# Two-layer hybrid decoder trunk on one core: a small tanh ahead of the gates, a swapped last step of the input projection, rotary key steps pinned, exponentials reordered

## The chip, the cores and the metric

The kernel runs on one core of one Trainium2 chip. The metric is the device time of one execution in microseconds (us), lower is better. The engines are named as in the profile: PE is TensorE (matmuls), DVE is VectorE, ACT is ScalarE, POOL is GpSimd, and SP issues the transfers.

## The reference

Two layers run over 256 tokens of width 1024. Each has a mixer sub-layer and a channel sub-layer; the change touches the mixer alone. Cut to what matters:

```
z = h @ w_in                        # one combined input projection of the normed x
q_lat, kv_lat, k_rope, qkv_b, conv_in, gate_logits = split(z)

q_a    = rms_norm(q_lat)  @ w_uq    # branch 1, MLA: 8 heads of 64 + 32 rotary
kv     = rms_norm(kv_lat) @ w_ukv
k_pe   = apply_rope(rms_norm(k_rope))                 # one rotary key, shared by the heads
o_a    = causal_attention(q_full, k_full, v_a) @ w_mla_o

o_b    = moba_attention(q_b, k_b, v_b) @ w_moba_o     # branch 2, here one block of 256 keys

glu_a, glu_g = split(conv_in)                         # branch 3, Conformer
u      = glu_a * sigmoid(glu_g)
u      = silu(layer_norm(causal_depthwise_conv(u, width 31)))
o_c    = u @ w_conv_pw2 + b

y      = (sigmoid(g0)*o_a + sigmoid(g1)*o_b + sigmoid(g2)*o_c) @ w_out
x      = x + g1 * y
```

`conv_in` is two times 512 channels wide. The latents (q_lat, kv_lat and k_rope) are together 672 wide. Sigmoid and silu are computed through tanh.

## The kernel before, in words

Every weight is float32 and is split by `split` into a rounded part (`whi`, made by ACT, L234) and a remainder (`wlo`, made by DVE, L235). A product then takes three matmuls (L324, L325, L327): `flush` issues the first two of every pair, and then the third of each. The weights come in units of up to 128x1024. `all_units` lists them in the order in which they are used, and `take` fetches and splits them a few units ahead of use (2 units in the input projection of layer 0, then 3). The four buffers `raw`, four `whi` and four `wlo` are taken in turn.

The code is written as one long sequence, but the order on each engine is drawn up when the kernel is built. A planner keeps one queue for each engine, follows the written order as a priority, and lets a later instruction go ahead where by its own estimate the earlier one's operands aren't there yet. What it drew up is fixed: on the chip each engine runs its list in order and waits where an operand is late. `tc.issue_after(i)` tells the planner to put an instruction behind `i` on the same engine.

The input projection of layer 0 is a loop over eight slices k of the model width. For each k, ACT and DVE make the normed and modulated slice: ACT `e` (L920) and its rounded copy `hh` (L921), DVE its remainder `hl` (L922). `latents(k)` multiplies it with the first 672 columns of the weights into three PSUM banks of the pool `psb` (`plat`, all three banks of the pool), and `conv_in(k)` with the 1024 columns of `conv_in` into four banks of the pool `psa` (`pci`, of five). `prepare_tile(k+1)` makes the next slice's gain and shift from 1024x1024 weights on DVE (L834) and is called between the two. At k = 2 the sine and cosine of the rotary angles are taken (L512), the only use of Sin. The other functions that ACT uses from there on are Tanh, Exp, Square, Copy and Identity.

After the loop, a written list of steps per layer, `STEPS`, sets the order. Layer 0 begins with `GLU0 GLU1 GLU2 GLU3 LE0 LE1 LR0 QKV00 LR1 LT QKV01 ...`:

- GLU: a tanh of one `pci` bank (L987, ACT) and its product with the other half (L988, DVE), into `upad`, the input of the width-31 convolution. It frees the bank.
- LE, LR, LT: the latents leave PSUM (L955 to L958, ACT), their squares are summed (L967, ACT) and raised to -1/2 (L545, POOL), and the latents are transposed (L975, PE) and split into the operands `qlh/qll` and `klh/kll` (L977 ACT, L978 DVE).
- QKV: the projection of the MoBA branch. Its first call takes two `psa` banks.
- UQ, UK, MS, MP: the up-projections of MLA, their norms, and the rotary steps. In `mla_prep` the shared rotary key `kr` is scaled (L1136) and turned (L1137, L1138, L678, L679).
- MA, BA: attention of four heads at a time through `attn4`. BA calls it with `apart=True`: the scores of the first 128 queries of heads 0 and 2 lie in a `psa` bank and those of heads 1 and 3 in a `psb` bank. Eight exponentials follow (L731, ACT), then two reciprocals (L736) and eight scalings (L743). The `p` buffers and the `smx` sums have four buffers each.
- V: the taps of the convolution (L1167, L1170, DVE), spread over most of the list; LN, LS, LB: the layer norm after it (L1180 to L1183 form its mean).
- C, G, O, OC, PR: gates and output projections; M and R: rows and columns of later modulations, from further weights (L432 on PE, L415 on DVE).

Layer 1 differs in that `conv_in` has the loop to itself and the latents follow as steps KL0 to KL7, behind the GLU steps.

Of the kernel before, what the change touches and what calls it, by code (L numbers as in the profile page):

```python
# [17 lines left out]
P = 128  # L18
# [142 lines left out]
def trunk_kernel(ctx, tc, xT, crow, ccol, pos, invf, modb_d, cols_d, grow_d, wmh, wmr, wm, win1, wqkv,  # L161
# [37 lines left out]
    def small(n, tag="sm", bufs=12):  # L199
        return wk.tile([P, n], F32, tag=tag, name=nm(tag), bufs=bufs)  # L200
# [60 lines left out]
    def all_units():  # L261
        for l in range(L):
            for k in range(KD):
                if l == 0:
                    yield win1[l, k, :, 0:672], [0], LEAD
                yield win1[l, k, :, 672:1696], [0], LEADS.get((l, "in", k), LEAD)
            for t in CFG["order"][l]:
                yield from ((*u, LEADS.get((l, *t), LEAD)) for u in token_units(l, t))
            if l == 1:
                for first in (0, NRAW):  # L270
                    for i in range(2):
                        for j in range(first, first + NRAW):
                            yield *chop(wup[l, j], KD, S)[i], LEADS.get((l, "up", j, i), LEAD)
            for up, j in FFN[l]:
                if up and l == 1 and j < 2 * NRAW:
                    continue
                for i, u in enumerate(chop(wup[l, j], KD, S) if up else chop(wdn[l, j], 1, 1024)):
                    yield *u, LEADS.get((l, "up", j, i), LEAD) if up else LEAD
# [403 lines left out]
    def attn4(qT, kT, v, scale, scq, oth, otl, oslot, apart=False):  # L682

        if apart:

            s0 = [psa(), psb()]
            at0 = [s0[h % 2][:, (h // 2) * P:(h // 2 + 1) * P] for h in range(4)]
        else:
            s0 = [psa()]
            at0 = [s0[0][:, (h % 2 * 2 + h // 2) * P:(h % 2 * 2 + h // 2 + 1) * P] for h in range(4)]  # L690
        s1 = [psa(), psa()]
        at1 = [s1[h % 2][:, (h // 2) * S:(h // 2 + 1) * S] for h in range(4)]
        for b, h in ((0, 0), (1, 1), (0, 2), (1, 3), (1, 0), (0, 1), (1, 2), (0, 3)):
            if b == 0:
                te.matmul(at0[h], qT(h)[:, 0:P], kT(h)[:, 0:P], start=(h == 0 or apart and h == 1), stop=False)
            else:
                te.matmul(at1[h], qT(h)[:, P:S], kT(h)[:, 0:S], start=(h < 2), stop=False)
        for t in s0:
            n = 2 if apart else 4
            te.matmul(t[:, 0:n * P].rearrange("p (h k) -> p h k", h=n), identb,  # L700
                      maskb.unsqueeze(1).to_broadcast([P, n, P]), start=False, stop=True)
        for t in s1:
            te.matmul(t.rearrange("p (h k) -> p h k", h=2)[:, :, P:S], identb,
                      maskb.unsqueeze(1).to_broadcast([P, 2, P]), start=False, stop=True)
        mx = small(8, "mx", 4).rearrange("p (b h) -> p b h", b=2)

        for i, t in enumerate(s0):
            n = 2 if apart else 4
            ve.tensor_reduce(mx[:, 0, n * i:n * i + n], t[:, 0:n * P].rearrange("p (h k) -> p h k", h=n), axis=AX.X,
                             op=ALU.max)  # L710
        for i, t in enumerate(s1):
            ve.tensor_reduce(mx[:, 1, 2 * i:2 * i + 2], t.rearrange("p (h k) -> p h k", h=2), axis=AX.X, op=ALU.max)
        nb = small(8, "nb", 4).rearrange("p (b h) -> p b h", b=2)
        if scq is None:
            ve.tensor_scalar(nb, mx, -scale, None, op0=ALU.mult)
        else:
            for b in range(NB):
                ve.scalar_tensor_tensor(nb[:, b, :], mx[:, b, :], -1.0, scq[b].rearrange("p (i j) -> p j i", i=2),
                                        op0=ALU.mult, op1=ALU.mult)
        yield  # L720
        prs = []
        for i in range(2):
            sm = small(4, "smx", 4)
            ps = []
            for h in (2 * i, 2 * i + 1):
                pr = wk.tile([P, 384], F32, tag="p", name=nm("p"), bufs=PB)
                for b in range(NB):
                    src = (at0 if b == 0 else at1)[h]
                    at = h % 2 * 2 + i
                    dst = pr[:, 0:P] if b == 0 else pr[:, P:384]  # L730
                    ac.activation(dst, src, AF.Exp, bias=nb[:, b, at:at + 1],  # L731
                                  scale=scale if scq is None else scq[b][:, h:h + 1],
                                  accum_out=sm[:, len(ps):len(ps) + 1])
                    ps.append(dst)
            ri = small(4, "ri", 4)
            ve.reciprocal(ri, sm)  # L736
            prs.append((ps, ri))
        for ps, ri in prs:
            for n, pr in enumerate(ps):
                if n in DVN:  # L740
                    ve.tensor_scalar(pr, pr, ri[:, n:n + 1], None, op0=ALU.mult)
                else:
                    ac.activation(pr, pr, AF.Copy, scale=ri[:, n:n + 1])  # L743
        yield
        pts = []
        slots = []
        for ps, _ in prs:
            slots += [ps[0], ps[1][:, 0:P], ps[1][:, P:S], ps[2], ps[3][:, 0:P], ps[3][:, P:S]]
            while len(slots) >= 4:
                pp = psa()  # L750
                for n in range(4):
                    te.transpose(pp[:, n * P:(n + 1) * P], slots[n], ident)  # L752
                slots = slots[4:]
                pt = operand([P, 512], "pT", "pT", 3, F32)
                ac.activation(pt, pp, AF.Copy)
                pts += [pt[:, n * P:(n + 1) * P] for n in range(4)]
        yield

        o = psa()
        for i in range(2):  # L760
            q0, q1 = slice(i * S, i * S + P), slice(i * S + P, i * S + S)
            for q, n, kb, start, stop in ((q0, 0, 0, True, True), (q1, 1, 0, True, False), (q1, 2, 1, False, True)):
                for j in range(2):
                    te.matmul(o[64 * j:64 * j + 64, q], v(2 * i + j, kb), pts[3 * (2 * i + j) + n], start=start,
                              stop=stop, tile_position=(0, 64 * j))
        oh = oth[:, oslot:oslot + 2, :].rearrange("p c t -> p (c t)")
        ac.activation(oh, o, AF.Copy)
        ve.tensor_tensor(otl[:, oslot:oslot + 2, :].rearrange("p c t -> p (c t)"), o, oh.bitcast(F32),
                         op=ALU.subtract)
# [27 lines left out]
    def layer(l):  # L797
# [112 lines left out]
        for k in range(KD):  # L910
            if l > 0:
                if k + 3 < KD:
                    tile(k + 3)
                hold[0] = [i.ins for i in tiles[-1]]
                conv_in(k)
                hold[0] = None
                mod_row(crow1[0], l, 2, k, scale=0.5 if CDMA else 1.0)
                continue
            t = e1()
            ac.activation(t, xn[k // 4][:, k % 4, :], AF.Identity, scale=gains[k], bias=sh1[:, k:k + 1])  # L920
            at = ac.activation(hh[:, k, :], t, AF.Copy)  # L921
            last = ve.tensor_tensor(hl[:, k, :], t, hh[:, k, :].bitcast(F32), op=ALU.subtract)  # L922
            if HOLD > 1:
                hold[0] = [last.ins]
            with tc.issue_after(wlast[0].ins) if k == 0 else ExitStack():
                latents(k)
            if k == 2:
                with tc.issue_after(at.ins):
                    step(trigs)
            if k + 1 < KD:  # L930
                prepare_tile(k + 1)
            conv_in(k)
            if k in C0K:
                gate_c(0, C0K[k], 3, psa)
            hold[0] = None
# [12 lines left out]
        qll = operand([P, 4, S], "lh1", "qll")  # L948
        klt = operand([P, 4, S], "obl", "klt")
        klh, kll = klt[:, 0:2, :], klt[:, 2:4, :]  # L950
        lats, lrs, krs = [], [], []

        def lat_evac(b):
            lat = ma(640)
# [15 lines left out]
        def lat_T():  # L970
            for n, gname, dh, dl, off in ((3, "q_g", qlh, qll, 0), (2, "kv_g", klh, kll, 384)):
                for c in range(n):
                    pt = psb()
                    for b in range(NB):
                        te.transpose(pt[:, b * P:(b + 1) * P], lats[b][:, off + c * P:off + (c + 1) * P], ident)  # L975
                    gcol = cv(l, gname)[:, c:c + 1]
                    ac.activation(dh[:, c, :], pt[:, 0:S], AF.Identity, scale=gcol)  # L977
                    ve.scalar_tensor_tensor(dl[:, c, :], pt[:, 0:S], gcol, dh[:, c, :].bitcast(F32),  # L978
                                            op0=ALU.mult, op1=ALU.subtract)


        upad = wk.tile([P, 4, S + 30], F32, tag="upad", name=nm("upad"), bufs=1)
# [136 lines left out]
        def mla_prep(b):  # L1119
# [13 lines left out]
            kf = ma().rearrange("p (h c) -> p h c", h=H)  # L1133
            ve.tensor_tensor(kf[:, :, 0:64], kn, krr.unsqueeze(2).to_broadcast([P, H, 64]), op=ALU.mult)
            kr = krs[b]
            ve.tensor_scalar(kr[:, 0:32], kr[:, 96:128], lrs[b][:, 2:3], None, op0=ALU.mult)  # L1136
            ve.tensor_tensor(kr[:, 32:64], kr[:, 0:32], ta[:, 0, b, 1, :], op=ALU.mult)  # L1137
            ve.tensor_tensor(kr[:, 64:96], kr[:, 0:32], ta[:, 1, b, 1, :], op=ALU.mult)  # L1138
            rope(kr[:, 0:16], kr[:, 16:32], kr[:, 32:64], kr[:, 64:96], 16)
# [454 lines left out]
```

## Time and profile before

| what | value |
|---|---|
| median of 3 runs | 900.23 us (899.14 to 901.38) |
| the profiled execution | 901.1 us, of which its span is 899.0 us |
| busy: PE, DVE, ACT, POOL | 877.8, 810.1, 557.8, 47.1 us |
| transfers | 201.59 MB, mean 224 GB/s |
| granted TensorE clock, mean | 0.996 |

The span is what the profiler recorded, from the first instruction of the program to its last. Busy time counts the stretches in which an engine has an instruction under way. An idle stretch is put down to what ended it. In the answers by time, each row is a start, a length, an engine, a line of the kernel, an operation and what it writes and reads; a bracket at the end gives the idle time ahead of it and who ended it.

### The profile page before, as it was taken

The page shows a single profiled execution, that of the slowest core. Times are in us where ns is not written, and L with a number is a line of the kernel's source. Part 1 is how long each engine was busy: PE and PEld are TensorE (multiplying, and loading weights), DVE is VectorE, ACT ScalarE, POOL GpSimd, SP SyncE. Part 2 cuts the span into 40 slices and gives each one's busy share as a digit, 9 for nine tenths or more (in the row PEclk, how much of TensorE's full clock was granted, in tenths as well). Part 3 has the DMA queues.
Part 4 walks back from the last instruction along what each step waited for, and adds up shares of the span by engine and source line. Part 5 has one row for each costly group of instructions (what it writes and reads, how often), then busy time and mean ns, then how long its engine had stood idle before and what let it go on. Part 6 is the DMA issues. An engine that isn't in the chain of part 4 may idle for free.

```text
span 899.0 us, 18558 instructions
## 1 busy us (share of the span) xinstructions
PE 877.8 (98%) x7233; PEld 833.8 (93%) x7233; DVE 810.1 (90%) x1592; ACT 557.8 (62%) x998; POOL 47.1 (5%) x36
## 2 busy tenths in 40 slices
PE   7999999999999999999999999999999999999998
PEld 6888888998998999999979988989999999999998
DVE  6989999999988989999966999999987899999874
ACT  4677588734756645665535676887475676655651
POOL 1000700000000000000000043000000000000000
PEclk8999999999999999999999999999999999999999
DMA  8966634698988788889835565156866576887631
GB/s 316 370 210 201 199 118 160 215 313 306 327 290 302 250 267 308 285 281 298 272 99 155 187 215 183 50 186 231 269 206 207 155 233 189 281 264 241 191 94 48
DMA packets 57976, 201.59 MB, mean 224 GB/s; under 512 B 6944, under 2 KB 8480, under 8 KB 57888
## 3 DMA queue, kind: packets, MB, share of 16 engines
q1 hardware_dynamic: 57888, 200.41, 67.3%
q8 instruction: 57, 0.93, 0.4%
q14 instruction: 31, 0.25, 0.1%
HBM read 199.33 MB, written 1.05 MB: 223 GB/s over the span
## 4 chain that ended last, share of the span: by engine, by line
PE 65%; DVE 22%; DMA 5%; ACT 4%; issue 4%; SPq 0%; DVEq 0%; ACTq 0%
PE psb L324 13%; PE psb L325 13%; PE psb L327 12%; DVE wlo L235 7%; PE psa L327 6%; PE psa L325 6%; PE psa L324 6%; DVE cacc L1170 3%; DVE raw L415 3%; DVE e L1462 2%; ACT whi L234 2%; DVE raw L834 1%; DMA raw<-in_win 1%; PE psa L432 1%; PE psa L752 1%
## 5 line engine op out<-in xcount | busy, mean ns | idle before, releaser
L234 ACT ACTIVATE whi<-raw 128x1024 fp32r<-128x1024 f32 (+2 forms) x286 | 295.3, 1041 | 182.4 <-PE psb L325 83.9
L235 DVE TENSOR_TENSOR wlo<-raw,whi 128x1024 fp32r<-128x1024 f32 (+2 forms) x286 | 340.0, 1193 | 37.5 <-ACT whi L234 29.8
L324 PE MATMUL psb<-hh,whi 128*128 128x256 f32 x1056 | 255.1, 282 | 1.0 <-ACT hh L633 0.5
L325 PE MATMUL psb<-hl,whi 128*128 128x256 f32 x1056 | 252.6, 280 | 0.0
L324 PEld LDWEIGHTS psb<-hh,whi 128*128 128x128 f32 x1056 | 198.6, 188 | 5.9 <-issue 2.8
L325 PEld LDWEIGHTS psb<-hl,whi 128*128 128x128 f32 x1056 | 198.7, 188 | 0.1
L327 PE MATMUL psb<-hh,wlo 128*128 128x256 f32 x1056 | 144.6, 278 | 0.0
L327 PEld LDWEIGHTS psb<-hh,wlo 128*128 128x128 f32 x1056 | 131.4, 188 | 0.4 <-issue 0.3
L1170 DVE SCALAR_TENSOR_TENSOR cacc<-upad,cw,cacc 128x256 f32<-128x256 f32 x240 | 105.5, 475 | 0.4
L324 PE MATMUL psa<-mhl,whi 128*128 128x256 f32 x400 | 93.4, 277 | 0.0
L325 PE MATMUL psa<-mhl,whi 128*128 128x256 f32 x400 | 93.2, 277 | 0.0
L1462 DVE SCALAR_TENSOR_TENSOR e<-psb,fw,e 128x255 f32<-128x255 f32 (+1 forms) x168 | 79.7, 476 | 6.4 <-ACT e L1460 5.6
L545 POOL TENSOR_TENSOR rs<-rs,mhalf 128x8 f32<-128x8 f32 (+3 forms) x26 | 45.5, 1762 | 673.3 <-DVE rs L544 673.2
L324 PEld LDWEIGHTS psa<-mhl,whi 128*128 128x128 f32 x400 | 74.9, 188 | 0.0
L325 PEld LDWEIGHTS psa<-mhl,whi 128*128 128x128 f32 x400 | 74.9, 188 | 0.0
L1460 ACT ACTIVATE e<-psb,fb,fw 128x256 f32<-128x256 f32 x84 | 46.5, 554 | 37.2 <-DVE e L1462 33.9
L415 DVE SCALAR_TENSOR_TENSOR raw<-raw,crow 128x1024 f32<-128x1024 f32 x56 | 67.9, 1216 | 0.8 <-DMA raw<-in_wmr 0.8
L327 PE MATMUL psa<-mhl,wlo 128*128 128x256 f32 x400 | 53.6, 276 | 0.0
L327 PEld LDWEIGHTS psa<-mhl,wlo 128*128 128x128 f32 x400 | 49.2, 188 | 0.0
L1470 ACT ACTIVATE mhl<-e 128x256 fp32r<-128x256 f32 x44 | 18.3, 416 | 30.9 <-DVE e L1468 29.3
L324 PE MATMUL psb<-whi,hh 128*128 128x416 f32 (+1 forms) x96 | 30.9, 349 | 3.0 <-ACT hh L921 3.0
L324 PE MATMUL psa<-hh,whi 128*128 128x256 f32 x128 | 29.7, 279 | 0.5 <-ACT hh L633 0.5
(295 smaller groups left out, 1515.4 us busy)
## 6 DMA issues: line engine op xcount, KB each, us to landing
raw<-in_wup SPq DMA_DIRECT2D x88, 512.0 KB, 4.9
raw<-in_wmr SPq DMA_DIRECT2D x68, 512.0 KB, 5.2
raw<-in_wdn SPq DMA_DIRECT2D x44, 512.0 KB, 4.6
raw<-in_wgab SPq DMA_DIRECT2D x32, 512.0 KB, 4.8
raw<-in_wqkv SPq DMA_DIRECT2D x24, 512.0 KB, 4.9
raw<-in_wm SPq DMA_DIRECT2D x24, 512.0 KB, 4.5
raw<-in_win SPq DMA_DIRECT2D x16, 512.0 KB, 5.5
raw<-in_wgc SPq DMA_DIRECT2D x16, 512.0 KB, 4.3
```

The lines of the kernel that those rows point to most:

```text
L234: ac.activation(hi, raw, AF.Copy)
L235: ve.tensor_tensor(lo, raw, hi.bitcast(F32), op=ALU.subtract)
L324: te.matmul(o, p1[0], p1[1], start=start, stop=False)
L325: te.matmul(o, p2[0], p2[1], start=False, stop=False)
L327: last = te.matmul(o, p3[0], p3[1], start=False, stop=stop)
L415: ve.scalar_tensor_tensor(raw, raw, scale, row, op0=ALU.mult, op1=ALU.mult, accum_out=acc)
L432: last = te.matmul(acc[32 * c:32 * c + 32, 0:S], cact[:, k:k + 1].to_broadcast([P, 32]), raw[:, c * S:(c + 1) * S], start=(k == 0), stop=( ...
L545: gp.tensor_tensor(r, r, mhalf[:, :n], op=ALU.pow)
L1170: ve.scalar_tensor_tensor(aj, upad[:, j, t:t + S], cw[:, j * 31 + t:j * 31 + t + 1], aj, op0=ALU.mult, op1=ALU.add)
L1460: ac.activation(t, src, AF.Identity, scale=fw[:, 2, c:c + 1], bias=fb[:, c:c + 1])
L1462: ve.scalar_tensor_tensor(t[:, d:S], src[:, 0:S - d], fw[:, 2 - d, c:c + 1], t[:, d:S], op0=ALU.mult, op1=ALU.add)
L1470: ac.activation(mh, th, AF.Copy)
```

## The change

Four edits, all of them to order or place. The arithmetic is the same, but for one added instruction whose result is not used.

1. In layer 0, a tanh of a 128x1 column into a small tile is put behind the copy `hh` (L921) of slice k = 4 on ACT.
2. In layer 0, at the last slice (k = 7), `conv_in` is called ahead of `latents`, and `all_units` lists the two units of that slice in the same order, so that the loads and splits swap with them.
3. In both layers, the first instruction on the rotary key (L1136) is to be issued behind the last `L978` of LT.
4. In `attn4`, the four `p` buffers and both sums are taken at the start, and with `apart=True` the exponentials of heads 1 and 3 on the first 128 queries (those in the `psb` bank) come first. The other six keep their order.

```diff
@@ all_units
             for k in range(KD):
+                two = [(win1[l, k, :, 672:1696], [0], LEADS.get((l, "in", k), LEAD))]
                 if l == 0:
-                    yield win1[l, k, :, 0:672], [0], LEAD
-                yield win1[l, k, :, 672:1696], [0], LEADS.get((l, "in", k), LEAD)
+                    two.insert(0 if k < KD - 1 else 1, (win1[l, k, :, 0:672], [0], LEAD))
+                yield from two
@@ attn4
+        sms = [small(4, "smx", 4) for _ in range(2)]
+        prt = [wk.tile([P, 384], F32, tag="p", name=nm("p"), bufs=PB) for _ in range(4)]
+
+        def exp(h, b):
+            at = h % 2 * 2 + h // 2
+            n = h % 2 * 2 + b
+            ac.activation(prt[h][:, 0:P] if b == 0 else prt[h][:, P:384], (at0 if b == 0 else at1)[h], AF.Exp,
+                          bias=nb[:, b, at:at + 1], scale=scale if scq is None else scq[b][:, h:h + 1],
+                          accum_out=sms[h // 2][:, n:n + 1])
+
+        first = [(1, 0), (3, 0)] if apart else []
+        for h, b in first:
+            exp(h, b)
         for i in range(2):
...
+                    if (h, b) not in first:
+                        exp(h, b)
...
@@ the loop over k
             with tc.issue_after(wlast[0].ins) if k == 0 else ExitStack():
-                latents(k)
+                if k < KD - 1:
+                    latents(k)
...
+            if k == 4:
+                with tc.issue_after(at.ins):
+                    ac.activation(small(1, "m0", 4), ones, AF.Tanh)
             if k + 1 < KD:
                 prepare_tile(k + 1)
             conv_in(k)
+            if k == KD - 1:
+                latents(k)
@@ lat_T
-                    ve.scalar_tensor_tensor(dl[:, c, :], pt[:, 0:S], gcol, dh[:, c, :].bitcast(F32),
-                                            op0=ALU.mult, op1=ALU.subtract)
+                    qparts.append(ve.scalar_tensor_tensor(dl[:, c, :], pt[:, 0:S], gcol, dh[:, c, :].bitcast(F32),
+                                                          op0=ALU.mult, op1=ALU.subtract))
@@ mla_prep
-            ve.tensor_scalar(kr[:, 0:32], kr[:, 96:128], lrs[b][:, 2:3], None, op0=ALU.mult)
+            with tc.issue_after(qparts[-1].ins):
+                ve.tensor_scalar(kr[:, 0:32], kr[:, 96:128], lrs[b][:, 2:3], None, op0=ALU.mult)
```

More of the change, by code (lines that the diff above doesn't have):

```diff
@@ L721, in attn4 @@
         prs = []
+        sms = [small(4, "smx", 4) for _ in range(2)]
[9 more added lines that the diff above has]
+            exp(h, b)
         for i in range(2):
-            sm = small(4, "smx", 4)
-            ps = []
             for h in (2 * i, 2 * i + 1):
-                pr = wk.tile([P, 384], F32, tag="p", name=nm("p"), bufs=PB)
                 for b in range(NB):
[L728 to L734, printed above, removed]
+                    if (h, b) not in first:
+                        exp(h, b)
             ri = small(4, "ri", 4)
-            ve.reciprocal(ri, sm)
-            prs.append((ps, ri))
+            ve.reciprocal(ri, sms[i])
+            prs.append(([prt[h][:, a:e] for h in (2 * i, 2 * i + 1) for a, e in ((0, P), (P, 384))], ri))
         for ps, ri in prs:
@@ L950, in layer @@
         klh, kll = klt[:, 0:2, :], klt[:, 2:4, :]
-        lats, lrs, krs = [], [], []
+        lats, lrs, krs, qparts = [], [], [], []
         def lat_evac(b):
```

## The prediction

> **What bounds the kernel now.** I read the busy shares first, then who waited for whom on PE and on DVE up to the end of layer 0's convolution, then busy time by stretch, and at last the single rows at the places that the edits touch.
>
> ```profile
> PE 877.8 (98%) x7233; PEld 833.8 (93%) x7233; DVE 810.1 (90%) x1592; ACT 557.8 (62%) x998; POOL 47.1 (5%) x36
> ...
> core 0: us, PE busy (x) PEld busy (x) DVE busy (x) ACT busy (x) POOL busy (x), PEclk, DMA share, GB/s
> ...
> 57.00:62.00 5.00, 3.93 (x31) 3.49 (x29) 2.87 (x10) 4.29 (x13) 0.00 (x0) 1.00 0.82 244
> 62.00:132.00 70.00, 69.83 (x412) 59.43 (x413) 69.66 (x144) 52.63 (x104) 20.95 (x10) 1.00 0.51 164
> ```
>
> PE is busy for 98% of the span, so an edit of order can only win back PE's waits. The stretches show a second engine at its limit: DVE is busy for 69.66 of the 70 us from 62 to 132. The one hole is 57 to 62 us, where PE is busy for 3.93 of 5 us and DVE for 2.87. That is the seam between the loop over k and the written list. The waits from 20 to 215 us, for PE and then for DVE, name its cause:
>
> ```profile
> PE psb L1183 <- DVE e L1182: 1.5, 1, 1.5
> PE psa L324 <- DVE upad L988: 1.1, 1, 1.1
> ...
> DVE wlo L235 <- ACT whi L234: 4.3, 9, 1.5
> DVE upad L988 <- ACT e L987: 2.1, 1, 2.1
> DVE ri L736 <- ACT p L731: 0.9, 1, 0.9
> ```
>
> The seam in order of time, ACT, then DVE, then PE:
>
> ```profile
> 57.68 0.49 ACT L955 ACTIVATE ma<-psb 128x384 f32<-128x384 f32 x1 [0.71 <-PE psb L327]
> 59.59 0.23 ACT L967 ACTIVATION_READ_ACCUMULATOR b<-ma 128x1 f32 x1
> 59.84 1.28 ACT L987 ACT_TABLE_LOAD   x1
> 61.13 1.21 ACT L987 ACTIVATE e<-psa 128x256 f32<-128x256 f32 x4
> ...
> 61.55 1.42 DVE L988 SCALAR_TENSOR_TENSOR upad<-e,psa 128x256 f32<-128x256 f32 x4 [2.13 <-ACT e L987]
> ...
> 57.29 0.78 PE L327 MATMUL psb<-wlo,hh 128*128 128x416 f32 x4
> 59.40 1.07 PE L327 MATMUL psa<-hh,wlo 128*128 128x256 f32 x8
> 60.30 0.39 PE L324 MATMUL psa<-whi,hh 128*128 128x512 f32 x1
> 62.03 0.50 PE L324 MATMUL psa<-whi,hh 128*128 128x512 f32 x1 [1.10 <-DVE upad L988]
> ```
>
> The latents of slice 7 end at 58.07, `conv_in` at 60.47. ACT has spent the time meanwhile on the latents' copies and first square, then loads a table (1.28 us, Sin to Tanh), and only at 61.13 takes the tanh of GLU0. The product frees the first bank, and the second bank of QKV00, which needs it, starts at 62.03 after a wait of 1.10 us. DVE has stood for 2.13 us.
>
> **The change part by part, against the profiled execution's 901.1 us.**
>
> *Edits 1 and 2, at the seam.* With `conv_in` first, the latents' twelve matmuls (six sums of 416 columns, six of 256) come between it and QKV00. Their last four and `conv_in`'s last eight are the two L327 rows above; by the starts of the matmul rows in the loop, a latents call takes about 1.8 us of PE. So `conv_in` ends about 1.8 us earlier, at 58.6, and GLU0 needs one tanh (a quarter of 1.21, with its start-up about 0.4) and one product (about 0.4): it ends near 59.5 if the table is there, 0.8 us before QKV00 wants the bank at 60.3. PE's 1.10 us goes. With the swap alone the table load would still stand ahead of the tanh, and the bank would come free near 60.8. DVE, free from 59.42, finds its first product ready: of its 2.13 us some 0.1 stays.
>
> What it moves: two transfers, two ACT splits and two DVE remainders swap. The rows ahead of the seam:
>
> ```profile
> 49.10 0.75 ACT L234 ACTIVATE whi<-raw 128x672 fp32r<-128x672 f32 x1
> 49.76 0.40 ACT L921 ACTIVATE hh<-e 128x256 fp32r<-128x256 f32 x1
> 50.61 1.07 ACT L234 ACTIVATE whi<-raw 128x1024 fp32r<-128x1024 f32 x1 [0.45 <-DMA raw<-in_win]
> ...
> 49.89 0.86 DVE L235 TENSOR_TENSOR wlo<-raw,whi 128x672 fp32r<-128x672 f32 x1 [0.20 <-ACT whi L234]
> 50.66 0.42 DVE L922 TENSOR_TENSOR hl<-e,hh 128x256 fp32r<-128x256 f32 x1
> 54.84 1.22 DVE L235 TENSOR_TENSOR wlo<-raw,whi 128x1024 fp32r<-128x1024 f32 x1
> 55.97 0.42 DVE L922 TENSOR_TENSOR hl<-e,hh 128x256 fp32r<-128x256 f32 x1
> ```
>
> The larger unit now stands where the 672-wide one stood: ACT has it 0.32 us longer ahead of `hh` of slice 6, DVE 0.36 us longer ahead of `hl` and all that follows for slice 7. The remainder in front of the last `hl` is 0.36 us shorter in return. Between 0 and 0.68 us later, I take 0.3. On SP the two transfers only change places in a queue that waits for buffers either way; both bring the same bytes, and the larger one is asked for first.
>
> Behind it: the copies of the latents start near 60.9 instead of 57.68, and LR, LT and UQ follow. PE needs the transposes after QKV00, about 63.4; the six copies (57.68 to 59.33 before) end at 62.6. POOL's two powers for the latents start later with LR, and their readers stand far behind (the first scaled copy of UQ, at 75.62). ACT loses about 3 us of early work and sheds the 1.28 us load. Its cover is its share in 62 to 132 us, 52.63 of 70.
>
> *The tanh of edit 1* costs a load and a small activation on ACT behind `hh` of slice 4:
>
> ```profile
> 38.93 0.41 ACT L921 ACTIVATE hh<-e 128x256 fp32r<-128x256 f32 x1
> 41.49 1.07 ACT L234 ACTIVATE whi<-raw 128x1024 fp32r<-128x1024 f32 x1 [2.15 <-DMA raw<-in_win]
> 43.18 0.60 ACT L920 ACTIVATE e<-mq,mod,gs 128x256 f32<-128x256 f32 x1 [0.63 <-DVE gs L841]
> ```
>
> ACT stands for 2.15 us there, from 39.34. The load, 1.28, and a tanh of one column (about 0.2 by the smallest activations in the seam, the 0.23 us accumulator read) fit. Without that cover the split at 41.49 would come up to 1.5 us late, of which the 0.63 us wait behind it takes part. I cost it at nothing.
>
> "ScalarE: Activation LUTs" in the Trainium skill (section "What ACT_TABLE_LOAD costs") has a drain of about 1.38 us with each load, about 2.66 us in all. The trace disagrees at the seam: the read before the load ends at 59.82, the load starts at 59.84 and the tanh at 61.13. By the page the added load would overfill the gap of 2.15 us; by the rows it leaves 0.7 us.
>
> *Edit 3.* Five small steps for each half of the tokens move back on DVE, in layer 0 from among the `L978` splits:
>
> ```profile
> 66.98 0.23 DVE L1136 TENSOR_SCALAR kr<-kr,rs 128x32 f32<-128x32 f32 x1
> 67.13 0.47 DVE L978 SCALAR_TENSOR_TENSOR qll<-psb,col,qlh 128x256 fp32r<-128x256 f32 x1
> 68.69 0.87 DVE L978 SCALAR_TENSOR_TENSOR klt<-psb,col,klt 128x256 fp32r<-128x256 f32 x2
> ...
> 65.11 1.76 POOL L545 TENSOR_TENSOR rs<-rs,mhalf 128x3 f32<-128x3 f32 x1 [53.44 <-DVE rs L544]
> ```
>
> The first reads the power that POOL ends at 66.87 and stands 0.11 us behind it. With the latents late it would hold DVE; behind LT it doesn't. UQ starts on PE at 73.8, four us after the last split, so nothing waits on this now: no gain, no loss, within 0.2 us. In layer 1 the key steps (first at 517.2) already run behind LT (last split ends at 514.9).
>
> *Edit 4.* The `psb` bank of heads 1 and 3 is free after two of the eight exponentials instead of seven, some 2.7 us earlier. The one PE wait for it in layer 0 is at 161.38:
>
> ```profile
> 160.77 0.47 ACT L731 ACTIVATE p<-psb,nb,rs 128x128 f32<-128x128 f32 x1
> 161.12 0.21 ACT L731 ACTIVATION_READ_ACCUMULATOR p<-psb,nb,rs 128x1 f32 x1
> 161.38 0.39 PE L324 MATMUL psb<-hh,whi 128*128 128x256 f32 x1
> ...
> PE psb L1183 <- DVE mod L416: 1.0, 1, 1.0
> PE psb L324 <- ACT p L731: 0.2, 1, 0.2
> ```
>
> PE's row before ends at 161.25 by its model, a loss of about 0.2 to 0.3 us; layer 1 has one more of that size (the last two lines are PE's waits from 480 to 640 us). Both lie ahead of a PE wait for the convolution's mean (1.5 us in layer 0, 1.0 in layer 1), which DVE sets. What PE gains there it waits for later. I take 0, with 0.5 us as the other end.
>
> *The sum.* At the seam PE gains 1.1 − 0.3 = 0.8 us and DVE 2.0 − 0.3 = 1.7. DVE has no idle time to speak of up to its wait for exponentials at 132 (0.9 us), and the mean at 213.68 goes by DVE. DVE hands its gain on only as far as PE and ACT keep up, so the gain is between 0.8 and 1.7 there: I take 1.3. Behind that the same work follows 1.3 us earlier. 901.1 − 1.3 = 899.8 us. The median of the runs, 900.23, is 0.87 under the profiled execution, so I forecast 898.9.
>
> **The rivals.** A change of 0.3% (2.7 us) is about what a measurement can tell from none; forecast and most rivals are inside it.
>
> *More than the seam (−3.4 us, 896.8).* DVE's 1.7 us come through whole, the exponentials bring their 0.5, and the planner, which draws all of layer 0's later queues anew, puts the mean's last sum ahead of a row product, 1.2:
>
> ```profile
> 211.96 1.23 DVE L415 SCALAR_TENSOR_TENSOR raw<-raw,crow 128x1024 f32<-128x1024 f32 x1
> 213.11 0.43 DVE L1182 TENSOR_TENSOR e<-e,e 128x256 f32<-128x256 f32 x1
> 213.68 0.67 PE L1183 MATMUL psb<-e,mean_w 128*128 128x256 f32 x2 [1.55 <-DVE e L1182]
> ```
>
> For it: this 1.23 us stands between the sum's operands (ready 211.98) and the sum. Against: nothing in the change aims at it.
>
> *The gain is spent (900.2).* The same redraw can as well put one more 1.2 us instruction ahead of the mean, or PE's wait for exponentials at 132 grows by what DVE gained. Then the seam closes and the end stands still.
>
> *The added load isn't covered (899.6).* If the load takes as long as the page has it, ACT's split of slice 5 is about 0.7 us late and DVE's chain with it: 0.7 us of the 1.3 is lost.
>
> *Slower: the late latents hold PE at the transposes (903.8).* PE reaches them near 63.4. ACT has from 60.9 the six copies, the LR squares of both halves, four tanh and two 1.08 us splits to do, 7.4 us by their rows. If the planner puts the copies last, they end at 68.3 and PE stands for 4.9 us. It decides when the copies come more than 1.3 us late. Against: the copies are written right behind GLU, ahead of the squares.
>
> **How the numbers follow.** Forecast case 0.50, spent 0.19, load not covered 0.03, more 0.22, slower 0.06. Faster by over 0.3% (below 897.5) has 0.22; the forecast, the spent gain and the load are within 0.3%, 0.72; slower 0.06. The range leaves out the slow rival and the far end of the better one: from 896.4 (DVE's whole 2.1 us, 0.5 for the exponentials and the 1.23 us row) to 901.4, the spent case with one more 1.2 us instruction in the way. The forecast case alone reaches from 898.0 (1.7 and the exponentials' 0.5) to 899.8 (0.8, and 0.38 more lost to the swapped splits).
>
> **What the changed profile would show.** Right: no table load at the seam but one near 39 to 43 us; GLU0 done before the latents end; no PE wait for `upad` and DVE's 2.1 us gone; QKV00 one piece, near 60.6; the key steps behind `klt`; two `psb` exponentials first, and no PE wait for `p` on `psb`. PE's wait for the mean goes down in layer 0 and up in layer 1. Wrong: PE waits for `ma` copies ahead of L975, `hl` of slice 7 more than 0.7 us later, or a longer DVE wait for exponentials near 131.

## The result, and the profile after

| kernel | median, us | lowest to highest | ratio to before (95% interval) |
|---|---|---|---|
| before, beside the first runs of the change | 899.59 | 898.50 to 901.38 (6 runs) | 1 |
| changed, first runs | 904.81 | 903.26 to 907.99 (6 runs) | 1.0056 [1.0041, 1.0071] |
| changed, later runs (experiment 11) | 905.75 | 901.18 to 911.03 (12 runs) | 1.0059 [1.0037, 1.0081] |

The forecast was 898.9 us, within a range from 896.4 to 901.4, no change that could be told. The change costs about 5 us, and its own runs lie farther apart than those of the kernel before: its twelve later runs spread over 9.9 us, 29 runs of the kernel before beside them over 7.0. The profiled execution of the changed kernel took 906.9 us, with a span of 904.8.

The shares of the span, from the page:

```profile
PE 880.2 (97%) x7233; PEld 835.8 (92%) x7233; DVE 810.9 (90%) x1592; ACT 559.7 (62%) x999; POOL 50.5 (6%) x36
```

The busy time by stretch; the columns are the stretch, its length, the busy time of PE, PE's weight loads, DVE, ACT and POOL with their instructions in brackets, and then the granted clock, the DMA share and GB/s:

```profile
57.00:62.00 5.00, 5.00 (x38) 4.72 (x36) 3.99 (x14) 2.85 (x8) 0.00 (x0) 1.00 0.75 225
62.00:132.00 70.00, 66.63 (x362) 56.20 (x361) 63.16 (x133) 48.05 (x97) 24.39 (x10) 0.95 0.44 146
106.00:110.00 4.00, 0.98 (x8) 0.78 (x6) 4.00 (x7) 3.40 (x5) 2.14 (x2) 0.96 0.49 159
110.00:116.00 6.00, 6.00 (x20) 4.87 (x20) 3.24 (x9) 0.72 (x2) 5.43 (x3) 0.50 0.39 125
```

The stretch that I had watched, 57 to 62, is now full. The loss is in the next one, which I had taken as given: DVE is busy there for 63.16 us where it was 69.66, PE for 66.63 where it was 69.83, and the granted clock is 0.95. Two rows inside it say where: from 106 to 110 PE works for 0.98 of 4 us, and from 110 to 116 it runs at half clock. One figure on the busy line fits in: POOL's few instructions took 50.5 us where they took 47.1.

PE's waits and DVE's, from 20 to 215 us:

```profile
PE psa L696 <- ACT qkT L1165: 3.0, 1, 3.0
PE psb L325 <- ACT hh L927: 2.6, 2, 2.0
PE psa L325 <- ACT whi L234: 1.8, 1, 1.8
...
DVE wlo L235 <- ACT whi L234: 4.6, 10, 1.2
DVE ma L1134 <- POOL rs L546: 2.8, 1, 2.8
```

The waits for `upad` are gone from both lists. In their place PE waits for a split (`whi`, L234) and, later, for the latent attention's copies (`qkT`, L1165); DVE waits for a power on POOL (`rs`, L546), which was in no list before.

**The seam, in order of time** (PE, then ACT, then DVE):

```profile
53.06 1.07 PE L328 MATMUL psa<-hh,wlo 128*128 128x256 f32 x8
55.98 0.50 PE L325 MATMUL psa<-whi,hh 128*128 128x512 f32 x1 [1.85 <-ACT whi L234]
59.14 1.07 PE L328 MATMUL psa<-hh,wlo 128*128 128x256 f32 x8
60.78 0.78 PE L328 MATMUL psb<-wlo,hh 128*128 128x416 f32 x4
...
38.95 1.28 ACT L939 ACT_TABLE_LOAD   x1
54.38 0.60 ACT L926 ACTIVATE e<-mq,mod,gs 128x256 f32<-128x256 f32 x1 [3.52 <-DVE gs L847]
54.88 1.04 ACT L234 ACTIVATE whi<-raw 128x1024 fp32r<-128x1024 f32 x1
55.83 0.40 ACT L927 ACTIVATE hh<-e 128x256 fp32r<-128x256 f32 x1
...
60.44 1.23 DVE L235 TENSOR_TENSOR wlo<-raw,whi 128x1024 fp32r<-128x1024 f32 x1 [1.01 <-ACT whi L234]
61.58 1.41 DVE L1000 SCALAR_TENSOR_TENSOR upad<-e,psa 128x256 f32<-128x256 f32 x4
```

The tanh's load lies at 38.95, in idle time. But a split of QKV00's first unit now stands on ACT between `e` and `hh` of slice 7, so `hh` begins at 55.83 where it began at 54.64, and PE has nothing to do for 1.85 us up to 55.98. DVE's product into `upad` begins at 61.58; before it was 61.55. A remainder (`wlo`) of QKV00's third unit stands in front of it now.

**The power on POOL, and what hangs on it.** First the changed kernel (POOL, DVE, PE), then the kernel before (POOL, PE):

```profile
92.86 7.84 POOL L546 TENSOR_TENSOR rs<-rs,mhalf 128x16 f32<-128x16 f32 x1 [0.35 <-DVE rs L545]
...
97.65 0.29 DVE L1153 COPY ma<-kr 128x256 f32<-128x256 f32 x1
100.73 0.69 DVE L1134 TENSOR_TENSOR ma<-ma,rs 128x512 f32<-128x512 f32 x1 [2.79 <-POOL rs L546]
...
104.12 1.03 PE L1164 MATMUL psa<-ident,ma 128*96 128x128 f32 x8
106.33 0.36 PE L325 MATMUL psb<-hh,whi 128*128 128x256 f32 x1
109.71 2.08 PE L696 MATMUL psa<-qkT 96*128 96x128 f32 x8 [3.02 <-ACT qkT L1165]
112.01 3.62 PE L698 MATMUL psa<-qkT 96*128 96x256 f32 x8
115.85 1.35 PE L1164 MATMUL psa<-ident,ma 128*96 128x128 f32 x8
```

```profile
93.94 3.34 POOL L545 TENSOR_TENSOR rs<-rs,mhalf 128x16 f32<-128x16 f32 x1
...
105.07 1.91 PE L1151 MATMUL psa<-ident,ma 128*96 128x128 f32 x16
107.58 1.16 PE L695 MATMUL psa<-qkT 96*128 96x128 f32 x8
108.80 1.89 PE L697 MATMUL psa<-qkT 96*128 96x256 f32 x8
110.74 1.04 PE L1151 MATMUL psa<-ident,ma 128*96 128x128 f32 x8
```

The changed kernel reaches the first transposes of the latent attention (L1164, L1151 before) 0.95 us ahead, at 104.12. It reaches the second pair's transposes 5.11 us behind, at 115.85 instead of 110.74. In between the same instruction on the same 128x16 numbers took 7.84 us on POOL instead of 3.34. DVE stood for it, 2.79 us. ACT has the copies of the transposed heads (`qkT`, L1165) behind a step that needs a sum of DVE's (L1066); it stood 4.77 us for that sum and made the copies only from 108.52. PE stood for 3.0 us, and then the same sixteen score products and masks (L696 to L704) took 6.14 us (109.71 to 115.85) instead of 3.16, at half clock. The end of the kernel shows the same distance: 906.9 − 901.1 = 5.8 us between the two profiled executions.

### The profile page after: what moved, and what is told of

Read it like the earlier page. It is cut to its first block, busy times and chain, and to the rows that moved or that the text cites. A ratio compares the mean times of both kernels' runs of the same rounds, so it can differ in the third digit from the quotient of the medians.

```text
span 904.8 us, 18555 instructions
## 1 busy us (share of the span) xinstructions
PE 880.2 (97%) x7233; PEld 835.8 (92%) x7233; DVE 810.9 (90%) x1592; ACT 559.7 (62%) x999; POOL 50.5 (6%) x36
## 4 chain that ended last, share of the span: by engine, by line
PE 75%; DVE 13%; DMA 5%; ACT 4%; issue 2%; POOL 1%; SPq 0%; DVEq 0%; ACTq 0%
PE psb L325 15%; PE psb L326 14%; PE psb L328 14%; PE psa L328 8%; PE psa L326 7%; PE psa L325 7%; DVE wlo L235 4%; DVE cacc L1183 3%; ACT whi L234 2%; DMA raw<-in_wup 2%; PE psa L433 1%; POOL rs L546 1%; PE psa L758 1%; DMA raw<-in_win 1%; PE psa L770 1%
## 5 line engine op out<-in xcount | busy, mean ns | idle before, releaser
L234 ACT ACTIVATE whi<-raw 128x1024 fp32r<-128x1024 f32 (+2 forms) x286 | 295.5, 1042 | 188.7 <-PE psb L326 89.5
L546 POOL TENSOR_TENSOR rs<-rs,mhalf 128x8 f32<-128x8 f32 (+3 forms) x26 | 49.0, 1897 | 676.5 <-DVE rs L545 676.5
```

Source lines behind the costliest of these rows:

```text
L234: ac.activation(hi, raw, AF.Copy)
L546: gp.tensor_tensor(r, r, mhalf[:, :n], op=ALU.pow)
```

## The experiments

The theory after the first comparison: the swap makes the planner draw VectorE's queue anew behind the second pair of `rs` steps, into a run of steps with two inputs in SBUF each; while these follow each other, POOL's power can't read its operands; so it comes late, PE gets a hole, and the hole costs clock as well. Rivals: the late latents themselves, another edit, the seam, or just an odd execution.

**1 and 2. The swap alone, and all but the swap.** Experiment 1 is the kernel before with this edit only; experiment 2 has the other three edits and not this one:

```
- if l == 0: yield win1[l, k, :, 0:672], ...        # latents' unit first
- yield win1[l, k, :, 672:1696], ...
+ two = [conv unit]; two.insert(0 if k < KD - 1 else 1, latents' unit)
+ yield from two
...
+ if k < KD - 1: latents(k)        ...  conv_in(k)
+ if k == KD - 1: latents(k)
```

> Edit 2 alone: conv_in ahead of the latents at the last slice, with its two units swapped; no early tanh, old key steps, old order of the exponentials. Port theory: the swap alone redraws DVE's queue behind the second pair of rs steps (both key-and-query scalings back to back, no split between them), POOL's 16-wide power waits for its operands until DVE stands (a row of 4 to 8 us instead of 3.3), PE stands about 3 us ahead of the first MLA scores and runs them at half clock: slower than before by 3 to 8 us. Rival, exponentials: the loss belongs to edit 4, so this is within 1.5 us of before or faster. Rival, late latents: the transposes and UQ are late at 63 to 75 us and PE waits there.

> Edits 1, 3 and 4 without the swap. Port theory: DVE's queue behind the second pair of rs steps is that of before, the 16-wide power takes 3 to 3.5 us, PE has no 3 us hole at the MLA scores: within 1.5 us of before, with the table load gone from the seam and up to 1 us gained there. Exponentials theory: the 5 us loss is here too.

Measured: the swap alone 907.27 us, ratio 1.0081 [1.0061, 1.01]; the other three 900.41 us, ratio 1.0001 [0.9987, 1.0014]. The loss is the swap's, and the other three edits together change nothing in the time that can be measured. They do change the seam. By stretch, and then at the transposes of the latents, experiment 2 shows:

```profile
57.00:62.00 5.00, 5.00 (x36) 4.51 (x35) 4.19 (x14) 4.64 (x16) 0.00 (x0) 1.00 0.79 245
...
62.84 0.82 PE L983 MATMUL psb<-ident,ma 128*128 128x128 f32 x6
```

The early tanh closes PE's hole without the swap. In the kernel before, these transposes start at 64.44, so PE is 1.60 us ahead, of which 0.33 stood already at the last products of slice 6's `conv_in` (53.69 against 54.02). That is a gain of about 1.3 us at the seam, the size that I had forecast, and it doesn't reach the end. At the convolution's mean in layer 1 PE is 0.82 us ahead (629.76 against 630.58), and its wait there is 1.81 us instead of 1.02.

The swap alone, first by stretch, then ACT at the seam and POOL in order of time:

```profile
57.00:62.00 5.00, 5.00 (x29) 4.88 (x28) 2.81 (x11) 1.36 (x2) 0.00 (x0) 0.66 0.75 221
```

```profile
62.29 1.28 ACT L991 ACT_TABLE_LOAD   x1
...
96.90 6.29 POOL L546 TENSOR_TENSOR rs<-rs,mhalf 128x16 f32<-128x16 f32 x1 [0.33 <-DVE rs L545]
```

The long power is there again. New is the first row: behind a hole of 1.80 us at the seam the granted clock is 0.66 over 5 us. By that share I estimate 3.4 us at half clock, which would cost PE 1.7 us. And without the early tanh the table load stands ahead of GLU at 62.29; that the swap alone was the slowest kernel of all fits that, but nothing tried it by itself. In this execution the clock also fell once in layer 1 (0.62 over 719 to 723 us).

**3 and 4. One step more on VectorE, with one input or with two.** Both are the changed kernel with one step that nobody reads, right behind the second pair of `rs` steps, as long in the one as in the other (0.68 us):

```
+ with tc.issue_after(rst[0].ins):                      # layer 0, second half
+     ve.tensor_reduce(door, x[:, 0:2, :] ..., op=ALU.add)          # 3: one input
+     ve.tensor_tensor(b2(), x[:, 0:2, :], x[:, 2:4, :], op=ALU.add) # 4: two inputs
```

> The changed kernel with one added DVE step behind the second pair of rs steps in layer 0: a sum over 128x512 of x, with one SBUF input, result unused, about 0.68 us. Port theory: POOL gets its operands during it, the second 16-wide power takes about 2.8 us from its start instead of 7.84, DVE doesn't wait for it, the hole ahead of the MLA scores and the half clock go: 3 to 6 us faster than the changed kernel, near or under before. Late-latents theory: the hole stays, as the power was late for its inputs: no faster than the changed kernel, 0.7 us slower at most.

> The control: the same place and length, but an addition of two 128x512 halves of x, two SBUF inputs. DVE's queue is otherwise that of the one-input kernel, step for step. Port theory: POOL is held at least through this step, so the power's row is 0.6 us or more longer than with the one-input step, and up to 8 us; the time is that of the changed kernel, or between. If any extra step helps by moving the queue alone, both kernels have the same power row and the same time.

Measured: 903.42 us, ratio 1.0032 [1.0019, 1.0045], with one input; 904.76 us, ratio 1.005 [1.0036, 1.0064], with two. VectorE's other steps stand in the same order in both. The power that is issued 0.09 us into the extra step, one input first:

```profile
95.46 0.68 DVE L1132 TENSOR_REDUCE door<-x 128x8 f32<-128x512 f32 x1
...
95.55 2.90 POOL L546 TENSOR_TENSOR rs<-rs,mhalf 128x16 f32<-128x16 f32 x1 [0.52 <-DVE rs L545]
```

```profile
94.91 0.69 DVE L1132 TENSOR_TENSOR b<-x 128x512 f32<-128x512 f32 x1
...
95.00 8.44 POOL L546 TENSOR_TENSOR rs<-rs,mhalf 128x16 f32<-128x16 f32 x1 [0.37 <-DVE rs L545]
```

2.90 us against 8.44, one execution of each: behind the one-input step the power has its way free, behind the two-input step it hasn't. What every execution repeats is the power of the first pair. In the changed order it is issued 0.05 to 0.07 us into a remainder with two inputs (86.92 to 88.15 in the changed kernel), and it took 3.92 to 3.94 us in all eight profiles that have it there. In the order of before it is issued beside a one-input sum, and it took 2.90 in both profiles (before and experiment 2). The changed kernel, then the kernel before:

```profile
86.97 3.94 POOL L546 TENSOR_TENSOR rs<-rs,mhalf 128x16 f32<-128x16 f32 x1 [19.28 <-DVE rs L545]
...
89.33 2.90 POOL L545 TENSOR_TENSOR rs<-rs,mhalf 128x16 f32<-128x16 f32 x1 [21.33 <-DVE rs L544]
```

In each of the eight the power ends 2.75 to 2.77 us behind the end of that remainder. The Trainium skill has the rule on the page "SBUF — State Buffer" (section "SBUF: two separate sides"): VectorE with two SBUF inputs, or in a two-port mode, and GpSimd reading SBUF want the same pair of ports, which is held for a whole instruction while the other side blocks. All these rows agree. The copy at 97.65 in the changed kernel agrees as well: it has one input, but the long power ends 2.76 us behind the copy's end, just as behind the remainders, and 2.96 behind the two-input step ahead of the copy; and the page counts an fp32 copy within SBUF among the two-port ones.

In time the two experiments aren't clear of each other, and the one-input step brought some 2.2 to 2.4 us against the changed kernel, by the ratios, where I had expected 3 to 6. It was still 0.32% slower than before, so the 16-wide power isn't all. Two things were left in its profile: the clock at the seam, 0.66 over 57 to 62 us in both, and the 8-wide power behind the freed one, which took 6.37 us and held DVE for 1.53. In experiment 4's profile the late power held DVE for 2.8 us, but PE has no hole ahead of the scores (3.71 of 4 us busy from 106 to 110), so a late power doesn't always cost PE at that place.

**5, 6 and 7. The seam's hole filled, the powers left out, and both.** All three leave the order of all other instructions on every engine as it is in the changed kernel. Where the powers are left out, the roots aren't taken, so the numbers behind them are not the kernel's:

```
+ with tc.issue_after(clast[KD - 2].ins):     # 5, 7: last product of slice 6's conv_in
+     warm(pqkv[0][0], 16)                    # 16 idle matmuls into QKV00's first bank
- gp.tensor_tensor(r, r, mhalf[:, :n], op=ALU.pow)     # 6, 7: not for q and k of layer 0's latents
```

> The changed kernel with 16 idle matmuls (ones by ones into the bank that the first QKV product then starts afresh) on TensorE behind the sixth conv product, where it waits 2.0 us for the split weights at 54 to 56 us; the order of everything else on every engine is unchanged. Theory 'two places': the hole at the seam often ends with TensorE at half clock at 57 to 62 us (granted 0.66 in the three experiments before), which costs some 1.7 us; filled, the clock there is 1.00 in the profile, the long wait of the power on POOL behind it is untouched (6 to 8 us), and the median falls by 1 to 2 us to 903 to 904. Rival 'the seam only shifts work' (the clock there costs nothing, since DVE sets the time behind it): median unchanged within 0.5 us. Rival 'all of the loss is at the seam': median at 900.5 or below.

> The changed kernel without layer 0's four powers on POOL (16 and 8 wide, both token halves): the values go on unrooted, so part of the computation is left out; the order of everything else on every engine is unchanged. Theory 'two places': DVE's 2.8 us wait for the second 16-wide power goes, TensorE's hole ahead of the latent attention's scores goes with it and so does the half clock behind the hole: 3 to 5 us off, median 900 to 902, still above the kernel before by the seam's clock (1 to 2 us). Rival 'the later latents themselves hold the transposes': the hole ahead of the scores stays and the median stays at 904 or more. Rival 'seam only': no change beyond 0.5 us.

> Both at once: the 16 idle matmuls in the seam's hole, and layer 0's four powers left out (the values go on unrooted). Theory 'two places': the two gains add, median 898.5 to 900.5, and what the swap gained at the seam shows: at or up to 1 us below the kernel before. Rival 'a third place': 901.5 or more, 1 us or more above the kernel before with no long TensorE hole ahead of 120 us in the profile. Rival 'they share one gain' (either alone brings all): no better than the better of the two alone.

| | powers as they are | powers left out |
|---|---|---|
| hole as it is | 1.0056 [1.0041, 1.0071] and 1.0059 [1.0037, 1.0081] | 902.35 us, 1.0018 [1.0006, 1.0029] |
| hole filled | 904.69 us, 1.0046 [1.0032, 1.006] | 900.68 us, 1.0003 [0.999, 1.0016] |

Without the powers some 0.4% is gone, 3.4 to 3.7 us; with the hole filled as well the median is another 0.15%, 1.3 us, lower, but there the two intervals overlap. With both, nothing that can be measured is left, so the medians ask for no third place; 0.16% could still hide in the interval. The powers' part is thus shown. That the seam's clock costs the rest is argued: the estimate of 1.7 us from its row, in five of the seven profiles that have the open hole, is of the right size. The fill alone brought 0.1%, inside the intervals, which is under what I had expected: its profile shows why. The clock at the seam is full, but the power still takes 6.30 us, PE gets a hole of 2.0 us ahead of the scores, and the clock falls there:

```profile
57.00:62.00 5.00, 5.00 (x38) 4.86 (x38) 3.99 (x13) 2.85 (x8) 0.00 (x0) 1.00 0.71 220
106.00:110.00 4.00, 2.01 (x11) 1.81 (x10) 4.00 (x10) 3.29 (x6) 3.56 (x2) 0.79 0.37 131
110.00:116.00 6.00, 6.00 (x23) 4.69 (x22) 3.26 (x7) 0.58 (x2) 4.00 (x3) 0.57 0.27 87
```

**8. A short one-input step.** As experiment 3, but the step takes 0.21 us and stands one step later, behind the first product with the 16-wide reciprocal:

```
+ first = ve.tensor_tensor(q3[:, :, 0:64], ...)
+ with tc.issue_after(first.ins): ve.tensor_reduce(door, x[:, 0, 0:64] ..., op=ALU.add)
```

> The changed kernel with one more short one-input step on VectorE (a 128x8 sum over 128x64 of x, about 0.15 us) right behind the first product with the 16-wide reciprocal of the first token half, so about 0.6 us after the second 16-wide power has been issued on POOL. Nothing reads it. Theory 'port': the power gets in at this step: 3.3 to 3.6 us in the profile instead of 6.3 to 8.4, no 2.8 us wait of VectorE for it; median 902 to 903.5, the rest of the loss being the seam's. Rival 'any break in the run of steps of its kind decides by chance' or 'the step is too short to let it in': the power takes 6 us or more, and the median is 904 to 905.

Measured: 901.91 us, ratio 1.0026 [1.0007, 1.0045], with runs from 899.45 to 909.0. The 16-wide power took 3.35 us, as expected. What I had not expected is that the 8-wide one behind it was caught instead, as it was in experiment 3. POOL by form from 92 to 105 us (busy time of the two, mean ns), and DVE's wait in order of time:

```profile
L546 POOL TENSOR_TENSOR rs<-rs,mhalf 128x8 f32<-128x8 f32 x2 | 7.8, 3878 | 0.0
```

```profile
104.96 0.69 DVE L1150 TENSOR_TENSOR ma<-kv,rs 128x512 f32<-128x512 f32 x1 [1.53 <-POOL rs L546]
```

The first of the two had its way free and took 1.64 us, so the second took 6.1. One gap let one power in. This profile is of the slowest of the twelve runs, 909.0 us, and not all of its loss is at the two places: the clock fell twice more in layer 1 (0.67 over 636 to 641 us, 0.58 over 719 to 723), the first time behind a wait of PE's of 2.4 us for DVE (`mod`, L417).

**9. The control: the kernel before without the same four powers.** The edit is that of experiment 6 on the kernel before; its order, too, is unchanged.

> The control to the run without powers: the kernel BEFORE the change without the same four powers of layer 0 on POOL (values unrooted, so part of the computation is left out); the order of everything else on every engine is unchanged. Theory 'the order decides': in the order of before these powers cost VectorE next to nothing (3.3 us and no wait), so nothing is gained: ratio 0.998 to 1.000, 898.5 to 900.5. Rival 'the powers cost every order the same' (the 3.4 us gained by leaving them out of the changed kernel are a general cost of POOL's work): 896.5 to 897.5, ratio 0.996 to 0.997.

Measured: 899.65 us, ratio 0.9991 [0.9976, 1.0005]. In the order of before these powers cost nothing that can be told; the 3.4 us of experiment 6 are no general price of work on POOL.

**10. The changed kernel whole, with two short one-input steps and the filled hole.** Experiment 8's step, one more like it behind the copy of the first half's rotary key, and experiment 5's matmuls.

> The changed kernel, whole, with two short one-input steps on VectorE (128x8 sums over 128x64 of x that nobody reads: one right behind the first product with the 16-wide reciprocal of the first token half, one behind the copy of its rotary key) and the 16 idle matmuls in the seam's hole. Theory 'port and clock': both powers of the second half get in early (16 wide 3.3 to 3.6 us, 8 wide under 3.5 instead of 6.1), no hole ahead of the scores, 1.00 at 57 to 62 us: ratio 0.9995 to 1.002, 899.5 to 902. It does not fall clearly below the kernel before, since the run without powers and with the hole filled did not. Rival 'the powers only move their stall' (a third one is caught, or the 8-wide one still is): a hole of 1 us or more ahead of the scores, ratio 1.003 or more.

Measured: 900.09 us, ratio 1.0001 [0.9988, 1.0015]. Both powers together take 5.02 us, and from 84 to 120 us neither PE nor DVE has a wait left in its list. POOL and PE's hole in order of time, then the stretches:

```profile
93.35 5.02 POOL L546 TENSOR_TENSOR rs<-rs,mhalf 128x16 f32<-128x16 f32 x2 [0.32 <-DVE rs L545]
...
54.51 1.92 PE L348 MATMUL psa<-warm_w 128*128 128x256 bf16 x16
```

```profile
57.00:60.00 3.00, 3.00 (x24) 2.90 (x24) 2.92 (x11) 0.82 (x2) 0.00 (x0) 1.00 0.77 250
110.00:116.00 6.00, 5.99 (x50) 4.96 (x49) 6.00 (x13) 4.82 (x17) 3.35 (x3) 1.00 0.19 61
```

The loss is repaired, with 18 instructions that compute nothing. But the repaired kernel is no faster than the kernel before: its first transposes come 0.42 us ahead (104.65), as much as it was ahead at slice 6's `conv_in` already (53.60 against 54.02), and by 250 us that is gone (249.66 against 249.46 at the next transposes). No experiment points to a version that beats both.

**11. The changed kernel again.**

> The changed kernel as it is, once more, beside the two others. What is open is the spread (903 to 908 in its first six runs). Theory 'chance at two doors': the 16-wide power of the second half takes 6 us or more again, and the clock at 57 to 62 us falls to 0.6 to 0.7 in some profiles and not in others; median 904 to 906, ratio 1.004 to 1.007. Rival 'the first profile was an odd one': the power takes under 4 us and the ratio is under 1.003.

Measured: 905.75 us, ratio 1.0059, runs from 901.18 to 911.03. Neither theory has it right. In this profiled execution, of the same program, the power got in early, and the clock fell at the seam:

```profile
95.00 0.42 DVE L1136 TENSOR_TENSOR ma<-ma,rs 128x256 f32<-128x256 f32 x1
95.34 1.24 DVE L235 TENSOR_TENSOR wlo<-raw,whi 128x1024 fp32r<-128x1024 f32 x1
...
94.49 3.69 POOL L546 TENSOR_TENSOR rs<-rs,mhalf 128x16 f32<-128x16 f32 x1 [0.33 <-DVE rs L545]
```

```profile
54.00:57.00 3.00, 1.21 (x7) 0.92 (x6) 3.00 (x11) 2.52 (x4) 0.00 (x0) 0.95 0.37 132
57.00:60.00 3.00, 3.00 (x14) 2.87 (x13) 2.53 (x11) 0.29 (x1) 0.00 (x0) 0.50 0.72 226
```

So both losses come and go from execution to execution of one program. Here PE was 0.80 us ahead of the kernel before at the end of slice 6's `conv_in` (53.22 against 54.02) and 0.78 behind at the latents' transposes (65.22 against 64.44), so the seam cost it about 1.6 us of the 2.7 between the two profiled executions; where the rest was lost isn't shown. A clear run of the power takes 2.90 us, so here it got in near 94.49 + 3.69 − 2.90 = 95.28, at the change from L1136 to the remainder at 95.34 (the stretch rows show the seam of this execution: the hole, then half clock). In the first profile the same two steps followed each other at 93.70 and the power stayed out. That the changed kernel's times spread over 10 us fits this, but two profiles don't show it.

## Why the prediction was wrong, point by point

- *Edits 1 and 2: no table load at the seam, no PE wait for `upad`.* Right. Right too that the added load is covered: it starts at 38.95 as `hh` ends, the tanh starts at 40.24 as it ends, and the split behind them waits for PE, not for the load.
- *"Between 0 and 0.68 us later, I take 0.3" for the swapped units.* Wrong in size. `e` of slice 7 came 0.37 us later, as the widths have it, but `hh` came 1.19 us later, because the redraw put a whole split of QKV00's first unit between the two. I had moved the two units within the old queue; that split was not in the sum. `hl` of slice 7 came 1.14 us later (57.11 against 55.97), and more than 0.7 was one of my signs of being wrong. `conv_in` ends at 60.21 by PE's row instead of the 58.6 I had worked out.
- *DVE's gain of 1.7 us.* It is nil: `upad` at 61.58 against 61.55. The remainder of QKV00's third unit, which before came behind the products (63.72), now stands in front of them (60.44).
- *PE's gain of 0.8 us.* It is nil too. PE is 0.95 us ahead at the first transposes of the latent attention, but it was 0.96 ahead already at the last products of slice 6's `conv_in` (53.06 against 54.02): what it gained on the wait for `upad` it lost in the hole.
- *QKV00 in one piece near 60.6.* Wrong: its first two matmuls run at 55.98, as the hole ends, one more at 57.53, the rest from 61.40.
- *The late latents.* The copies run from 61.37 and the transposes from 63.54; I had 60.9 and 63.4. The rival "slower" had its place here and its 4.9 us; nothing waits here. The kernel became slower at a place that no rival named.
- *Edits 3 and 4: 0.* The key steps run at 71.41, behind the last `klt` split, and PE's wait for an exponential on `psb` is gone from the list; experiment 2 has all but the swap at 1.0001. What I hadn't asked is what edit 1 does alone: experiment 2 has the seam's gain without the swap.
- *"Behind that the same work follows 1.3 us earlier."* This is the step that failed. I wrote myself that the planner draws all of layer 0's later queues anew, but priced the redraw at one place, the convolution's mean, and at one row of 1.2 us, in both directions. It cost 3.4 to 3.7 us at a place where the profile before shows no wait at all (experiments 6 and 9), and about 1.3 us that I put down to the clock behind a hole that the swap made (6 against 7, not clear of the spread). Together that is about the 5 us. The step fails even without the redraw's cost: in experiment 2 the seam's 1.3 us is there and the time is that of before, which is my rival "the gain is spent".
- The trace of before had a sign of the first. The same power on the same shape took 2.90 and 3.34 us, and the 8-wide one 1.64 and 2.67, as its rows from 89 to 100 us have it. An instruction whose length depends on what runs beside it is a wait that the profile books as busy time. I read those rows only for the latents' power at 65.11.

```profile
L545 POOL TENSOR_TENSOR rs<-rs,mhalf 128x16 f32<-128x16 f32 x2 | 6.2, 3122 | 21.4 <-DVE rs L544 21.3
L545 POOL TENSOR_TENSOR rs<-rs,mhalf 128x8 f32<-128x8 f32 x2 | 4.3, 2156 | 0.0
```

What stays open: why the power gets in at some changes from one two-input step to the next and not at others, and why the hole at the seam costs clock in some executions and not in all. The first bears on the theory: the kernel before has two-input steps behind the same power too (from 93.84 to 98.77), so by these few profiles the swap didn't make such a run, but an order in which the power gets in less often.

## What to carry to other kernels

Where a planner orders the queues, an edit's price isn't only in the rows that it touches: look behind it for instructions whose length depends on their neighbours, and for places where an engine has just no slack. In this kernel a power on GpSimd next to a full VectorE is such an instruction; it wants a one-input step on VectorE right where it is issued, and each power needs its own. A hole on TensorE is to be priced twice: for its length, and for the slow matmuls that can follow it. And a gain at one place is worth nothing until it has passed the next wait that another engine sets.

## What the runs showed of the hardware that was not expected

- POOL's 128x16 power takes 2.90 us with its way free and up to 8.44 beside back-to-back two-input steps. When it did get in between two of them (its end less 2.90 us), that was each time within 0.1 us of the start of a remainder step (`wlo`): 94.38 against 94.46 (before), 92.79 against 92.87 (experiment 2), 100.29 against 100.35 (experiment 1), 96.38 against 96.44 (experiment 5) and 95.28 against 95.34 (experiment 11). It does not get in at every such step.
- A hole of 1.8 us on TensorE can be followed by half clock for some 3.4 us (estimated from the shares below). At the seam, seven profiled executions with the hole left open had 1.79 to 1.85 us of it; five of them had a clock of 0.66 to 0.69 over 57 to 62 us, two 1.00, and all three with the hole filled had 1.00. Ahead of the latent attention's scores, four executions had a hole of 2.0 to 3.0 us, and all four had a clock of 0.50 to 0.72 over 110 to 116 us. The Trainium skill, "TensorE: Matmul & The Clock Gate" (section "What's actually happening"), has the clock fall after an idle window of about 3.4 us that runs freely. That the outcome changes from execution to execution agrees with a free window; that 1.8 us can be enough does not agree with the length.
